# RG-LRU gates as products of 64 rows with r and i side by side, and segment differences on GpSimd

## The chip, the cores and the metric

One core of a Trainium2 chip runs one program. The metric is the device time of an execution in microseconds (us); the kernel before takes 1347.77 us, the median of 3 runs (1346.13 to 1348.24). The engines are TensorE (PE; PEld is its weight load), VectorE (DVE), ScalarE (ACT), GpSimd (POOL) and SyncE (SP), which issues the DMAs here.

## What is computed

Two layers on x (1 x 512 x 1024, float32): a recurrent layer (an RG-LRU and a Mamba-2 SSD side by side, one input and one output projection), then dilated attention, each followed by a SwiGLU feed-forward. The change touches two places of the recurrent layer:

```python
xb = xc.reshape(b, l, LRU_BLOCKS, LRU_BLOCK)                    # 16 blocks of 64 channels
r = sigmoid(einsum('blhi,hij->blhj', xb, w_r).reshape(b, l, w) + b_r)
i = sigmoid(einsum('blhi,hij->blhj', xb, w_i).reshape(b, l, w) + b_i)
log_a = -LRU_C * r * softplus(-lam)
a, u = exp(log_a), sqrt(-expm1(2.0 * log_a)) * (i * xc)         # then a scan over time: h = a * h + u
...
seg = cs[:, :, :, None] - cs[:, :, None, :]                     # SSD, chunks of 128, 16 heads
decay = exp(where(causal, seg, -inf))
```

## The kernel before

Tiles are 128 partitions (channels) by 512 columns (time). The big projections (`project`, L231; L113 to L115) multiply in three passes of float32r: each weight tile of 128x1024 is loaded (`wr`), cast by ACT to `wh` and its rest `wl` is taken on DVE (`split`, L90 and L91). `weight(i)` issues loads and splits for two tiles ahead; there are three buffers each of `wr`, `wh` and `wl`. PSUM has four buffers for projections (`pa`) and three for all else (`pm`).

The recurrent layer works through 8 tiles of each kind. For RG-LRU tile j (called block j here, two of the reference's blocks of 64): projection, a convolution over time on DVE (`conv`, L292 and L295), then `lru_act(j)`: two float32 products with `lru_w`, whose 128x128 weight tile holds the two blocks of 64 on its diagonal and zeros elsewhere (L486 for r, L488 for i), Tanh of each (L491, L492), two Exps and a Tanh on ACT (L497 to L499) and two DVE steps (L500, L501). After every four blocks `lru_end` takes one Sqrt over all four (L563) and then, block by block, a product, the scan and the gate (L506, L510, L517) on DVE and a split.

For SSD heads, two at a time (`ssd_pair`): the running sum `cs` of a head is brought by DMA to all partitions (`bcs`), ACT takes its Exp for 64 rows of `E` (L536), four DVE instructions of 128x128 subtract the column's value and clip at 0 (L540), ACT takes Exp (L541), DVE multiplies by `cb` (L542). `ssd_out` uses the result as the moving operand of `ps_yd` (L552): for each chunk two products, whose outputs lie in the lower and the upper 64 partitions of one PSUM tile. `ps_yo` (L556) are whole products of 128 columns.

What follows a projection is put on the list `held` and issued after the matmuls of the next projection. The order on each engine is not the program's order: the tile framework's planner, with its own cost of every instruction, lets an engine take the earliest instruction in the program among those that it holds ready. On the chip, each engine then keeps that order.

```python
held.append(lambda: lru_act(j, xc))                       # in lru_gates(j), after project and conv
...
for j in range(8):
    lru_gates(j)
    if j % 2 == 1:
        ssd_pair(j // 2)
        gate(4 + j // 2)
    if j % 4 == 3:
        held.append(lambda j=j: lru_end(j))
```

The other four head pairs run later, between the z projections.

Of the kernel before, what the change touches and what calls it, by code (L numbers as in the profile page):

```python
# [10 lines left out]
F32 = mybir.dt.float32  # L11
F32R = mybir.dt.float32r
AF = mybir.ActivationFunctionType
ALU = mybir.AluOpType
AX = mybir.AxisListType

P = 128
D = 1024
T = 512
NT = T // P  # L20
KD = D // P
# [37 lines left out]
def trunk(ctx: ExitStack, tc: tile.TileContext, a):  # L59
    nc = tc.nc  # L60
    mm = nc.tensor.matmul
    V, S, G = nc.vector, nc.scalar, nc.gpsimd

    def fill(pool, n):
        t = pool.tile([P, n // 4], F32, name=f"fill{n}", bufs=1)
        nc.gpsimd.memset(t[:, :1], 0.0)
# [9 lines left out]
    pm = ctx.enter_context(tc.tile_pool(name="pm", bufs=3, space=bass.MemoryType.PSUM))  # L76
# [154 lines left out]
    def project(i, hl):  # L231
        w = weight(i)
        ps = pa.tile([P, T], F32, tag="pa", name="ps_pr")
        n = len(hl)
        for k in range(n):
            mm3(ps, w, hl[k], (slice(None), slice(k * P, (k + 1) * P)), (slice(None), slice(None)), k == 0, k == n - 1)
        ready = held[:]
        held.clear()
        for f in ready:
            f()  # L240
        return ps
# [13 lines left out]
        norm.feed_sq(k)  # L255
    with ExitStack() as rctx:
        rp = rctx.enter_context(tc.tile_pool(name="rp", bufs=1))
        lru_w = rp.tile([P, 2, KD, P], F32, name="lru_w")
        fill(rp, 320)
        hp = rctx.enter_context(tc.tile_pool(name="hp", bufs=1))  # L260
        sctx = ExitStack()
# [46 lines left out]
        for j in range(4):  # L308
            ps = first[j] if j < 2 else project(i_proj[32 + j], norm.hl)
# [8 lines left out]
        ps = pm.tile([P, T], F32, tag="pm", name="ps_dtt")  # L318
        W2 = 32 + H
        for c in range(NT):  # L320
# [22 lines left out]
        br2 = rp.tile([P, 8], F32, name="br2")  # L343
        bi2 = rp.tile([P, 8], F32, name="bi2")
# [9 lines left out]
            out=adt.rearrange("p (c h) -> p c h", c=NT),  # L354
            in0=dt.rearrange("p (c h) -> p c h", c=NT),
            scalar=-1.0,
            in1=ea.rearrange("p (o h) -> p o h", o=1).to_broadcast([P, NT, H]),
            op0=ALU.mult, op1=ALU.mult,
        )
        ps = pm.tile([P, T], F32, tag="pm", name="ps_cs")  # L360
# [10 lines left out]
        ps = pm.tile([P, T], F32, tag="pm", name="ps_csT")  # L371
# [10 lines left out]
        for g in range(2):  # L382
            ps = pm.tile([P, T], F32, tag="pm", name="ps_bt")
# [5 lines left out]
            ps = pm.tile([P, T], F32, tag="pm", name="ps_cb")  # L389
            for c in range(NT):  # L390
# [4 lines left out]
                out=t.rearrange("p (c l) -> p c l", c=NT), in0=ps.rearrange("p (c l) -> p c l", c=NT),  # L395
# [60 lines left out]
        for g in range(2):  # L456
            e_t = rt2.tile([P, NT - 1, T], F32, tag="xde", name=f"xde{g}", bufs=1)
            for jj in range(4):
                j = 4 * g + jj
                ps = project(i_proj[24 + j], norm.hl)  # L460
# [17 lines left out]
        def lru_gates(j):  # L478
            ps = project(i_proj[j], norm.hl)
            xc = rt2.tile([P, T], F32, tag="xc", name="xc", bufs=4)  # L480
            conv(ps, "lconv_w", "lconv_b", j, xc)
            held.append(lambda: lru_act(j, xc))

        def lru_act(j, xc):
            pr = pm.tile([P, T], F32, tag="pm", name="ps_r")
            mm(pr, lhsT=lru_w[:, 0, j], rhs=xc, start=True, stop=True)  # L486
            pi = pm.tile([P, T], F32, tag="pm", name="ps_i")
            mm(pi, lhsT=lru_w[:, 1, j], rhs=xc, start=True, stop=True)  # L488
            tr = rt2.tile([P, T], F32, tag="tr", name="tr", bufs=1)
            ti = rt2.tile([P, T], F32, tag="ti", name="ti", bufs=1)  # L490
            S.activation(tr, pr, AF.Tanh, scale=0.5, bias=br2[:, j:j + 1])  # L491
            S.activation(ti, pi, AF.Tanh, scale=0.5, bias=bi2[:, j:j + 1])  # L492
            av = rt2.tile([P, T], F32, tag="av", name="av", bufs=4)
            if j % 4 == 0:
                lru["a2"] = rt2.tile([P, 4, T], F32, tag="a2", name="a2", bufs=1)
            a2 = lru["a2"][:, j % 4]
            S.activation(av, tr, AF.Exp, scale=ch_[:, j:j + 1], bias=ch_[:, j:j + 1])  # L497
            S.activation(a2, tr, AF.Exp, scale=cf[:, j:j + 1], bias=cf[:, j:j + 1])
            S.activation(tr, tr, AF.Tanh, scale=chn[:, j:j + 1], bias=chn[:, j:j + 1])  # L499
            V.scalar_tensor_tensor(out=a2, in0=a2, scalar=1.0, in1=tr, op0=ALU.add, op1=ALU.mult)  # L500
            V.scalar_tensor_tensor(out=xc, in0=ti, scalar=1.0, in1=xc, op0=ALU.add, op1=ALU.mult)  # L501
            lru[j] = (av, a2, xc)
# [23 lines left out]
        ck3 = cst_.rearrange("p (c h) -> p c h", c=NT)  # L526

        def ssd_pair(j):
            g, jj = j // 4, j % 4
            E = sd.tile([P, T], F32, tag="E", name="E", bufs=1)  # L530
            MT = []
            for e in range(2):
                h = 2 * j + e
                bc = sd.tile([P, T], F32, tag="bcs", name="bcs", bufs=4)
                nc.sync.dma_start(out=bc, in_=csd[h:h + 1, :].to_broadcast([P, T]))
                S.activation(E[64 * e:64 * e + 64], bc[64 * e:64 * e + 64], AF.Exp)  # L536
                sg = bc
                for c in range(NT):
                    l = slice(c * P, (c + 1) * P)
                    V.tensor_scalar(out=sg[:, l], in0=bc[:, l], scalar1=ck3[:, c, h:h + 1], scalar2=0.0, op0=ALU.subtract, op1=ALU.min)  # L540
                S.activation(sg, sg, AF.Exp)  # L541
                V.tensor_tensor(out=sg, in0=sg, in1=CB[g], op=ALU.mult)  # L542
                MT.append(sg)
            held.append(lambda: ssd_out(j, E, MT))

        def ssd_out(j, E, MT):
            g, jj = j // 4, j % 4
            pd = pm.tile([P, T], F32, tag="pm", name="ps_yd")
            for c in range(NT):
                for e in range(2):  # L550
                    s = slice(c * P, (c + 1) * P)
                    mm(pd[64 * e:64 * e + 64, s], lhsT=xdt[j][:, c, 64 * e:64 * e + 64], rhs=MT[e][:, s], start=True, stop=True)  # L552
            po = pm.tile([P, T], F32, tag="pm", name="ps_yo")
            for c in range(1, NT):
                s = slice(c * P, (c + 1) * P)
                mm(po[:, s], lhsT=prev[g, c - 1][:, jj * P:(jj + 1) * P], rhs=CT[g][:, s], start=True, stop=True)  # L556
            V.tensor_tensor(out=E[:, P:], in0=E[:, P:], in1=po[:, P:], op=ALU.mult)
            V.scalar_tensor_tensor(out=xs[j], in0=xs[j], scalar=pc("ssd_d", j), in1=pd, op0=ALU.mult, op1=ALU.add)
            V.tensor_tensor(out=xs[j][:, P:], in0=xs[j][:, P:], in1=E[:, P:], op=ALU.add)
# [8 lines left out]
# [7 lines that stand above are left out]
# [41 lines left out]
        for j in range(8):  # L616
            if j >= 4:
                ssd_pair(j)
            if j == 0:
                ps = project(i_proj[16], norm.hl)  # L620
                lctx.close()
                zctx = ExitStack()
                rt2 = zctx.enter_context(tc.tile_pool(name="zp", bufs=2))
            else:
                ps = project(i_proj[16 + j], norm.hl)
            zz = zgate(j, ps)
            zlate(j, zz)
            if j >= 3:
                out_lru(j - 3)
# [18 lines left out]
        for m in range(8):  # L648
            ps = project(i_rec[1, m], ob)
# [38 lines left out]
    with ExitStack() as actx:  # L688
# [10 lines left out]
        for w, (gn, rn, scale) in enumerate((("q_gain", "q_rope", 0.125), ("k_gain", "k_rope", 1.0))):  # L699
            g = am.tile([P, 1], F32, name=f"gain{w}", bufs=1)  # L700
# [212 lines left out]
def _chan(v):  # L913

    return v.reshape(-1, P).T
# [77 lines left out]
```

## Time and profile before

| | us | note |
|---|---|---|
| median of 3 runs | 1347.77 | 1346.13 to 1348.24 |
| the profiled execution | 1346.39 | its span 1344.6 |
| PE busy | 1318.4 | 98% of the span |
| DVE busy | 796.2 | 59% |
| ACT busy | 573.4 | 43% |
| POOL busy | 151.7 | 11% |

The times in the rows below are microseconds from the start of the span unless marked ns. L486 is line 486 of the kernel before. Busy shares are averages over stages; what a wait costs is read where it stands. Neighbours in a timeline overlap a little, since an instruction's start is pipelined with the end of the one before.

### The profile page before, as it was taken

What the parts mean: (1) busy time and instruction counts of PE and PEld (TensorE: products, weight loads), DVE (VectorE), ACT (ScalarE), POOL (GpSimd) and SP (SyncE); (2) the same over time, 40 slices, a digit from 0 to 9 for tenths busy, and PEclk for the clock granted to TensorE, in tenths of its full rate; (3) what the DMA queues carried; (4) which work ended last, traced back from release to release, by engine and by line L of the source; (5) the groups of instructions that cost most, each with busy time, mean ns of one, the idle gap of its engine ahead of it and who ended that gap; (6) DMA issues with size and microseconds to landing.
All of it is one profiled execution on the core that took longest, in us unless ns stands there. A gap on an engine that the chain in (4) does not pass through costs nothing.

```text
span 1344.6 us, 15688 instructions
## 1 busy us (share of the span) xinstructions
PE 1318.4 (98%) x6058; PEld 1072.5 (80%) x6058; DVE 796.2 (59%) x1332; ACT 573.4 (43%) x842; POOL 151.7 (11%) x130
## 2 busy tenths in 40 slices
PE   8999989999999999999999999999999999999998
PEld 6877767788888888888888877777788888888887
DVE  6886799975454434434453778788764434443442
ACT  5743867443333222322243379558643212222321
POOL 0000000000000000000005755554300000000000
PEclk9999999999999999999999999999999999999999
DMA  6322222532323323233232221121032323323232
GB/s 239 111 80 93 95 79 71 174 101 94 94 94 94 95 96 102 89 106 94 89 100 94 90 68 47 63 78 48 32 108 96 94 95 96 100 87 110 94 95 78
DMA packets 38555, 126.50 MB, mean 94 GB/s; under 512 B 4289, under 2 KB 5057, under 8 KB 38353
## 3 DMA queue, kind: packets, MB, share of 16 engines
q1 hardware_dynamic: 38480, 125.51, 29.2%
q8 instruction: 47, 0.77, 0.2%
q14 instruction: 28, 0.22, 0.0%
HBM read 123.36 MB, written 2.13 MB: 93 GB/s over the span
## 4 chain that ended last, share of the span: by engine, by line
PE 81%; DVE 9%; ACT 6%; POOL 2%; issue 1%; DMA 0%; SPq 0%; POOLq 0%; DVEq 0%; ACTq 0%
PE ps_pr L113 24%; PE ps_pr L114 24%; PE ps_pr L115 24%; ACT s L825 2%; POOL qrs L757 1%; DVE q L758 1%; PE ps_qkv L738 1%; PE ps_qkv L737 1%; PE ps_qkv L736 1%; DVE q L766 1%; ACT ph L90 1%; PE ps_o L852 1%; PE ps_pT L845 1%; ACT qk_hi L783 1%; DVE rtmp L762 1%
## 5 line engine op out<-in xcount | busy, mean ns | idle before, releaser
L90 ACT CAST wh<-wr 128x1024 fp32r<-128x1024 f32 (+2 forms) x223 | 228.2, 1025 | 621.3 <-PE ps_pr L115 388.2
L113 PE MATMUL ps_pr<-xh,wl 128*128 128x512 f32 x1056 | 416.5, 395 | 12.7 <-DVE wl L91 12.0
L114 PE MATMUL ps_pr<-xl,wh 128*128 128x512 f32 x1056 | 414.5, 392 | 0.9 <-DVE xl L191 0.9
L115 PE MATMUL ps_pr<-xh,wh 128*128 128x512 f32 x1056 | 413.2, 391 | 0.0
L91 DVE TENSOR_TENSOR wl<-wr,wh 128x1024 fp32r<-128x1024 f32 (+2 forms) x191 | 225.6, 1182 | 52.3 <-ACT wh L90 51.9
L113 PEld LDWEIGHTS ps_pr<-xh,wl 128*128 128x128 f32 x1056 | 199.4, 189 | 55.5 <-DVE wl L91 12.9
L114 PEld LDWEIGHTS ps_pr<-xl,wh 128*128 128x128 f32 x1056 | 199.5, 189 | 43.5 <-DVE xl L191 1.8
L115 PEld LDWEIGHTS ps_pr<-xh,wh 128*128 128x128 f32 x1056 | 199.3, 189 | 42.4 <-issue 0.6
L113 PE MATMUL ps_pr<-ah,wl 128*128 128x512 f32 x352 | 136.9, 389 | 0.0
L114 PE MATMUL ps_pr<-al,wh 128*128 128x512 f32 x352 | 136.9, 389 | 0.0
L115 PE MATMUL ps_pr<-ah,wh 128*128 128x512 f32 x352 | 136.9, 389 | 0.0
L91 POOL TENSOR_TENSOR wl<-wr,wh 128x1024 fp32r<-128x1024 f32 x32 | 78.4, 2453 | 392.3 <-ACT wh L90 392.2
L670 DVE TENSOR_TENSOR tu<-ps_pr,nrb 128x512 f32<-128x512 f32 x44 | 30.4, 691 | 130.7 <-PE ps_pr L115 130.7
L678 DVE TENSOR_TENSOR x<-ps_pr,x 128x512 f32<-128x512 f32 x48 | 33.2, 692 | 120.4 <-PE ps_pr L115 120.3
L668 DVE TENSOR_TENSOR tg<-ps_pr,nrb 128x512 f32<-128x512 f32 x44 | 30.4, 691 | 94.1 <-PE ps_pr L115 94.1
L114 PEld LDWEIGHTS ps_pr<-al,wh 128*128 128x128 f32 x352 | 66.1, 188 | 13.8
L115 PEld LDWEIGHTS ps_pr<-ah,wh 128*128 128x128 f32 x352 | 66.1, 188 | 13.7
L113 PEld LDWEIGHTS ps_pr<-ah,wl 128*128 128x128 f32 x352 | 66.1, 188 | 13.7
L736 PE MATMUL ps_qkv<-wh,xl 128*128 128x512 f32 x192 | 75.6, 394 | 0.5 <-ACT q L750 0.5
L737 PE MATMUL ps_qkv<-wl,xh 128*128 128x512 f32 x192 | 75.5, 393 | 0.0
L738 PE MATMUL ps_qkv<-wh,xh 128*128 128x512 f32 x192 | 75.5, 393 | 0.0
L736 PEld LDWEIGHTS ps_qkv<-wh,xl 128*128 128x128 f32 x192 | 36.1, 188 | 7.9 <-ACT q L750 1.0
(233 smaller groups left out, 1575.2 us busy)
## 6 DMA issues: line engine op xcount, KB each, us to landing
wr<-in_w_gu SPq DMA_DIRECT2D x88, 512.0 KB, 3.5
wr<-in_w_in SPq DMA_DIRECT2D x35, 512.0 KB, 3.5
wr<-in_w_dn SPq DMA_DIRECT2D x32, 448.0 KB, 3.2
wr<-in_w_qkv SPq DMA_DIRECT2D x24, 512.0 KB, 3.5
wr<-in_w_out SPq DMA_DIRECT2D x16, 512.0 KB, 3.5
wr<-in_w_dn SPq DMA_DIRECT2D x16, 512.0 KB, 3.4
x<-in_xT SPq DMA_DIRECT2D x16, 256.0 KB, 3.7
bcs<-csd SPq DMA_DIRECT2D x16, 256.0 KB, 4.4
```

The costliest lines, as they stand in the source:

```text
L90: S.copy(hi, src)
L91: eng.tensor_tensor(out=lo, in0=src, in1=hi.bitcast(F32), op=ALU.subtract)
L113: mm(ps, lhsT=wl[ws], rhs=xh[xs], start=start, stop=False)
L114: mm(ps, lhsT=wh[ws], rhs=xl[xs], start=False, stop=False)
L115: mm(ps, lhsT=wh[ws], rhs=xh[xs], start=False, stop=stop)
L668: V.tensor_tensor(out=tg, in0=pg, in1=rb, op=ALU.mult)
L670: V.tensor_tensor(out=tu, in0=pu, in1=rb, op=ALU.mult)
L678: V.tensor_tensor(out=x[m], in0=ps, in1=x[m], op=ALU.add)
L736: mm(pss[t], lhsT=xl[:, ts_], rhs=wh[:, cols], start=(k == 0), stop=False)
L737: mm(pss[t], lhsT=xh[:, ts_], rhs=wl[:, cols], start=False, stop=False)
L738: mm(pss[t], lhsT=xh[:, ts_], rhs=wh[:, cols], start=False, stop=(k == KD - 1))
L825: S.activation(s, s, AF.Exp, scale=-1.0, bias=m[:, 0:1], accum_out=m[:, 1:2])
```

## The change

The weight tile of block j is now 64 rows for each of its two blocks, with r and i beside each other in the columns: rows 0 to 63 hold (w_r, w_i) of the first block, rows 64 to 127 hold (w_i, w_r) of the second. Each product has 64 rows and gives r of one block in one half of the partitions and i in the other, in its own PSUM tile. Tanh is taken half by half: `tr` from the halves that hold r, `ti` across the halves. The bias of i is stored with its halves exchanged. `lru_w` is half as large. And the four segment differences of each head are issued on POOL (`G`) and no longer on DVE (`V`).

```diff
-        lru_w = rp.tile([P, 2, KD, P], F32, name="lru_w")
+        lru_w = rp.tile([P, KD, P], F32, name="lru_w")
...
-            pr = pm.tile([P, T], F32, tag="pm", name="ps_r")
-            mm(pr, lhsT=lru_w[:, 0, j], rhs=xc, start=True, stop=True)
-            pi = pm.tile([P, T], F32, tag="pm", name="ps_i")
-            mm(pi, lhsT=lru_w[:, 1, j], rhs=xc, start=True, stop=True)
+
+            ps = [pm.tile([P, T], F32, tag="pm", name="ps_ri") for _ in range(2)]
+            own = [slice(64 * e, 64 * e + 64) for e in range(2)]
+            for e in range(2):
+                mm(ps[e], lhsT=lru_w[own[e], j], rhs=xc[own[e]], start=True, stop=True)
             tr = rt2.tile([P, T], F32, tag="tr", name="tr", bufs=1)
             ti = rt2.tile([P, T], F32, tag="ti", name="ti", bufs=1)
-            S.activation(tr, pr, AF.Tanh, scale=0.5, bias=br2[:, j:j + 1])
-            S.activation(ti, pi, AF.Tanh, scale=0.5, bias=bi2[:, j:j + 1])
+            for e in range(2):
+                S.activation(tr[own[e]], ps[e][own[e]], AF.Tanh, scale=0.5, bias=br2[own[e], j:j + 1])
+            for e in range(2):
+                o = own[1 - e]
+                S.activation(ti[own[e]], ps[e][o], AF.Tanh, scale=0.5, bias=bi2[o, j:j + 1])
...
-    blk = np.zeros((2, 8, P, P), f)
-    for g, w in enumerate((n["lru_w_r"][0], n["lru_w_i"][0])):
-        for b in range(16):
-            o = 64 * (b % 2)
-            blk[g, b // 2, o:o + 64, o:o + 64] = w[b]
+    w_r, w_i = (n[k][0].reshape(8, 2, 64, 64) for k in ("lru_w_r", "lru_w_i"))
+
+    blk = np.concatenate([np.concatenate([w_r[:, 0], w_i[:, 0]], axis=2), np.concatenate([w_i[:, 1], w_r[:, 1]], axis=2)], axis=1)
...
-                    V.tensor_scalar(out=sg[:, l], in0=bc[:, l], scalar1=ck3[:, c, h:h + 1], scalar2=0.0, op0=ALU.subtract, op1=ALU.min)
+                    G.tensor_scalar(out=sg[:, l], in0=bc[:, l], scalar1=ck3[:, c, h:h + 1], scalar2=0.0, op0=ALU.subtract, op1=ALU.min)
```

## Rows read from the trace of the kernel before

**Rows 1.** Busy time by stretches: the stretch, its length, busy time (and instructions) of each engine, granted clock.

```profile
134.20:148.70 14.50, 14.50 (x73) 10.80 (x73) 10.71 (x18) 14.36 (x18) 0.00 (x0) 1.00 0.24 73
148.70:157.80 9.10, 9.10 (x37) 6.55 (x36) 9.05 (x18) 5.76 (x10) 0.00 (x0) 1.00 0.14 58
157.80:170.50 12.70, 12.70 (x68) 9.71 (x67) 7.50 (x17) 12.56 (x15) 0.00 (x0) 1.00 0.41 126
...
189.50:217.80 28.30, 28.30 (x138) 20.45 (x137) 25.40 (x44) 27.31 (x35) 0.00 (x0) 1.00 0.40 130
...
229.00:330.00 101.00, 100.71 (x508) 82.55 (x509) 77.30 (x133) 42.48 (x61) 2.02 (x2) 1.00 0.39 125
```

**Rows 2.** Waits, 55 to 300: who waited for whom, us in total, times, longest.

```profile
PE ps_pr L113 <- DVE wl L91: 6.1, 2, 4.6
...
PEld ps_yd L552 <- ACT ti L492: 1.5, 2, 0.8
...
ACT tr L491 <- DVE a L500: 0.6, 1, 0.6
```

**Rows 3.** Chain of waits: start, us on the chain, what.

```profile
168.60 1.93 ACT a L563
...
181.12 1.15 DVE wl L91
182.31 0.80 PE ps_pr L113
...
209.18 0.58 ACT tr L491
...
215.86 1.93 ACT a L563
...
228.97 0.50 PE ps_pr L113
```

**Rows 4.** The same view, products of TensorE.

```profile
137.06 0.86 PE ps_i L488 x2
137.92 1.02 PE ps_yd L552 x16
140.30 0.67 PE ps_yo L556 x6
...
275.75 0.86 PE ps_yo L556 x6
```

**Rows 5.** Timeline of TensorE: start, us from first start to last end, instruction, count.

```profile
137.85 0.33 PE L552 MATMUL ps_yd<-bcs,xdt 128*64 128x128 f32 x2
```

**Rows 6.** Groups of ACT's instructions, 126 to 300: count, busy us, mean ns.

```profile
L536 ACT ACTIVATE E<-bcs 64x512 f32<-64x512 f32 x14 | 8.8, 629 | 10.0 <-DVE xs L559 9.8
L541 ACT ACTIVATE bcs<-bcs 128x512 f32<-128x512 f32 x14 | 8.7, 628 | 1.6 <-DVE bcs L540 1.5
```

**Rows 7.** Timeline of DVE.

```profile
205.67 1.26 DVE L540 TENSOR_SCALAR bcs<-bcs,csk 128x128 f32<-128x128 f32 x6
```

**Rows 8.** Groups of POOL's instructions by form.

```profile
L827 POOL TENSOR_SCALAR s<-s,m 128x384 f32<-128x384 f32 x16 | 9.8, 610 | 6.3 <-DVE m L826 4.8 <-ACT ph L90 1.5
...
L827 POOL TENSOR_SCALAR s<-s,m 128x128 f32<-128x128 f32 x16 | 6.4, 399 | 8.1 <-DVE m L826 8.1
```

**Rows 9.** Timeline of ACT.

```profile
201.84 0.63 ACT L536 ACTIVATE E<-bcs 64x512 f32<-64x512 f32 x1
...
207.11 1.14 ACT L541 ACTIVATE bcs<-bcs 128x512 f32<-128x512 f32 x2
...
214.57 1.28 ACT L563 ACT_TABLE_LOAD   x1
```

**Rows 10.** Timelines of POOL and of DVE in the attention.

```profile
744.23 2.88 DVE L758 TENSOR_TENSOR q<-q,qrs 128x512 f32<-128x512 f32 x1 [1.53 <-POOL qrs L757]
...
834.68 0.67 DVE L758 TENSOR_TENSOR q<-q,qrs 128x512 f32<-128x512 f32 x1
...
834.85 0.95 POOL L827 TENSOR_SCALAR s<-s,m 128x384 f32<-128x384 f32 x1 [0.17 <-DVE m L826]
```

**Rows 11.** Busy time by stretches, columns as in rows 1.

```profile
182.30:185.20 2.90, 2.89 (x7) 2.31 (x8) 2.90 (x6) 0.00 (x0) 0.00 (x0) 0.50 0.48 175
```

More of the change, by code (lines that the diff above doesn't have):

```diff
@@ L961 @@
         "lconv_w": conv(n["lru_conv_w"][0]), "lconv_b": _chan(n["lru_conv_b"][0]),
-        "b_r": _chan(n["lru_b_r"][0]), "b_i": _chan(n["lru_b_i"][0]), "lam": _chan(n["lru_lambda"][0]),
+        "b_r": _chan(n["lru_b_r"][0]), "b_i": _chan(n["lru_b_i"][0].reshape(8, 2, 64)[:, ::-1].reshape(-1)), "lam": _chan(n["lru_lambda"][0]),
         "sconv_w": conv(n["ssd_conv_w"][0]), "sconv_b": _chan(n["ssd_conv_b"][0]),
@@ L975 @@
         "w_dt": w_in[:, 4608:].reshape(8, P, 16).transpose(1, 0, 2),
-        "lru_w": blk.transpose(2, 0, 1, 3),
+        "lru_w": blk.transpose(1, 0, 2),
         "w_out": np.stack([_tiles(n["rec_w_out"][0][h * D:(h + 1) * D], 8) for h in range(2)]),
```

## The prediction

> **What bounds the kernel now.** The page's busy times, in the table above, come first: TensorE is busy 98% of the span, so a microsecond counts only if it shortens TensorE's work or one of its waits. Then the busy time by stretches, where the changed lines run. TensorE is full nearly everywhere, but ScalarE (ACT) is busy 14.36 of 14.50 us while blocks 0 and 1 of the RG-LRU go through, 12.56 of 12.70 around block 3 and 27.31 of 28.30 for blocks 4 to 7; between, from 148.7 to 157.8, it has 3.3 us of air. After 229 TensorE has next to none (100.71 of 101) [rows 1]. The waits tell where these stages touch TensorE: two waits, 4.6 and 1.5 us, for `wl`, the low part of a weight tile, made on VectorE (DVE) [rows 2]. The chain of waits shows what lies behind both: a run of ACT work ends in the Sqrt of L563, the scans of four blocks follow on DVE, `wl` stands among their last, and TensorE goes on at 182.31 and 228.97 [rows 3]. In this stage the path is ACT, then DVE; TensorE's products beside it are cover.
>
> **The change, step by step.** *Products.* A float32 product of 512 columns is two passes, 0.86 us in the chain, so r and i of a block cost 1.72 us [rows 4]. The new ones use 64 rows each, on different halves. The nearest row is `ps_yd`, on halves of the columns: two passes that take 0.33 us each are over in 0.33 us together [rows 5], and its sixteen take 1.02 us, where six whole passes of the same length (`ps_yo`) take 0.67, 0.11 each. Eight slots of 0.11 make 0.88, so 0.14 is entry; leaving costs 0.19, the difference between `ps_yo` right behind `ps_yd` (0.86) and elsewhere (0.67) [rows 4]. If halves of the rows run as halves of the columns do, a block costs 0.86 + 0.14 + 0.19 = 1.19 us, 0.53 less. In blocks 1, 3 and 7 the products stand right before `ps_yd`, which pays the way out already (rows 4 begin with one of the three): there it is 0.72. Blocks 4 and 5 come back to back before `ps_yd` and save 3.44 - 1.86 = 1.58. Together 3 x 0.53 + 3 x 0.72 + 1.58 = 5.3 us of TensorE work. Bounds: if nothing overlaps, entry and exit are added, 3 x 0.33 + 4 x 0.14 = +1.6 us; if of four passes only the middle two overlap, the saving is 5.3 - 8 x 0.43 = 1.9. I take 5.3, because the nearest row has pairs.
>
> By the Trainium skill, "TensorE: Matmul & The Clock Gate", section "Part 3: Packing small matmuls — row/col tiling", products on different rows of the array run at once, but matmuls start and end strictly in program order. If both passes of one half are issued before those of the other, that rule gives the saving of 1.9 us; `ps_yd` shows pairs from its first two passes on, and no row here shows a half of the rows.
>
> *Tanh.* Two activations per block become four, on 64 partitions each. Partitions don't set the time: 64x512 takes 629 ns on average, 128x512 628 [rows 6]. Back to back, a Tanh out of PSUM moves the chain by 0.58 us [rows 3], so a block adds 1.16 us to ACT, and all eight 9.3. Where do they lie? Blocks 0 to 2 add 3.5 us between 134 and 157.8, where ACT has 0.14 + 3.34 us of air [rows 1]; TensorE is a little ahead by then, so the air can be used, and next to nothing is late. Block 3 is in a full stretch: its Sqrt comes some 1.4 us later. The scans behind it are DVE work that loses nothing by the change, so `wl` and TensorE's restart move with it, to about 183.7. Blocks 4 to 7 add 4.64 us where there is 1.0 of air [rows 1], of which 0.6 is ACT's own wait for `a` (`tr` has one buffer) and is filled [rows 2]; 4.1 stay. The second Sqrt is late by 1.4 + 4.1 = 5.5 us, and with it the scans, `wl` and TensorE's restart at 228.97.
>
> *Segment differences.* 64 instructions leave DVE, at 0.21 us each (six in a row take 1.26) [rows 7]: 13.4 us of DVE time. On the path there is none of it: no L540 lies between a Sqrt and the `wl` after it, and the eight pieces of heads 6 and 7, the last of them in rows 7, are done while ACT is busy. On GpSimd (POOL) the nearest instruction, the attention's TENSOR_SCALAR of 128x128, takes 399 ns [rows 8]; eight are 3.2 us. ACT's Exp of `E` for head 7 starts at 201.84 and the Exps of the differences at 207.11 [rows 9]: 5.3 us, so POOL is hidden. The upper bound of a piece: a 128x384 one took 0.95 us beside a DVE product that read two inputs from SBUF, 0.34 more than the mean of its form [rows 8, 10]; with that on each, eight make 5.9 us, 0.6 more than the cover. Lower than nothing it can't be on this path, since ACT sets it. After 229 TensorE waits for next to nothing [rows 1], so the DVE time saved in the other eight heads brings nothing; the small `pow` of the group norm, on POOL too, could queue behind two pieces, 0.8 us.
>
> *Halved `lru_w`.* It is loaded once, long before its first use at 133 us, and nothing waits for it: nothing.
>
> **Sum.** TensorE's 5.3 us lie in front of two waits that others end: it arrives earlier and stands longer. Behind 229 it is full, so what counts is the second restart: +5.5 us. Then the clock. TensorE's idle 4.6 us before 182.31 [rows 2] was followed by 2.9 us at a granted clock of 0.50, the lower level (1.2 GHz) [rows 11], which costs 1.45 us. With TensorE 2.8 us quicker over blocks 4 to 7 (0.53 + 0.72 + 1.58) and the restart 4.1 us later against the first, the second idle becomes 1.5 + 2.8 + 4.1 = 8.4 us, and in one piece would bring another fall, +1.45. I leave that out of the value, because part of it should be spent earlier in short waits: the PSUM tiles of r and i are now held to the third and fourth Tanh, and `ps_yd` already waited for the end of `ti` [rows 2]. The profiled execution, 1346.4 us, goes to 1351.9; the median lies 1.4 above it, so I forecast **1353.3 us**, for this case alone 1350.8 (+3, if the planner uses more of ACT's air) to 1357 (+9, with the clock and POOL's 0.6 and 0.8).
>
> **Rivals.**
> 1. *TensorE's saving shows (not slower).* Where `wl` stands among the scans is planned, not given. If with Sqrt later the planner puts the second `wl` ahead of the scans, TensorE doesn't wait there and goes by its own work: first restart +1.4, blocks 4 to 7 -2.8, second wait -1.5: -2.9 on 1347.8, 1344.9 us. If the first `wl` moves too, that wait shrinks as well, but block 7's products still stand behind ACT and DVE, so not far below 1341. For it: DVE waits for Sqrt in both places, and `wl` would fit there. Against: in both places the cast that `wl` needs came behind Sqrt on ACT, and a fuller ACT has fewer gaps. It decides once that cast stands ahead of Sqrt.
> 2. *ACT takes them up (no change).* Four table loads of 1.28 us, the last of them in rows 9, lie in the stretch of blocks 4 to 7. If ACT's new order saves one there and one around block 3, and uses all air, the second restart is 5.5 - 2.6 - 0.4 = 2.5 us late; if the PSUM waits split the idle so that no clock falls at all, 1.45 comes back: +1.0, about 1348.8 us.
> 3. *POOL and DVE block one another (slower still).* A DVE product with both inputs in SBUF took 2.88 us beside a TENSOR_TENSOR on POOL, where another of the same form took 0.67 [rows 10]. If each of the eight pieces at 201 to 207 holds a DVE instruction for its 0.40 us, the DVE steps between ACT's are 3.2 us late in the full stretch: 5.5 + 3.2, 1356.5 us. It decides if TENSOR_SCALAR shuts DVE out as TENSOR_TENSOR does; the 0.67 was taken beside the piece of 0.95, so there POOL waited and DVE did not.
>
> The Trainium skill's "GPSIMD Engine Reference", section "8. Key points", says that POOL contends with DVE instructions that have two SBUF inputs, which most of DVE's here have; by it rival 3 would hold. Rows 10 agree for TENSOR_TENSOR, and for TENSOR_SCALAR only on POOL's side.
>
> **How the numbers follow.** Forecast 0.5, rival 1 0.2, rival 2 0.2, rival 3 0.1. A difference of 0.2%, 2.7 us, is about what a measurement of this kernel tells from no change; the bounds are 1345.1 and 1350.5. Faster: 0.15 (three quarters of rival 1). Same: the rest of rival 1 (0.05) and most of rival 2 (0.18), 0.23. Slower: 0.62. The range, 1344.5 to 1357.5 us, leaves out the deeper half of rival 1 and the ends of forecast and rival 3.
>
> **What would show it.** The products: four passes of 64 rows per block, starting in pairs 0.43 us apart. Tanh: 32 of 64x512, ACT without air from 190 to 223, the Sqrts at about 170 and 221. TensorE's waits for `wl`: two, together above 12 us. POOL: 64 pieces, 25 us or more. I am wrong if `wl` stands ahead of the scans, if the second Sqrt starts before 219 us, or if TensorE waits elsewhere before 330 us for more than 2 us.

## The result, and the profile after

The changed kernel takes 1379.39 us (median of 4 runs, 1378.06 to 1380.06), the kernel before beside it 1346.95 us (4 runs, 1346.13 to 1348.24): a ratio of 1.0233, 95% interval 1.0219 to 1.0248. The forecast was 1353.3 us with a range up to 1357.5: the sign was right, the size wrong by a factor of nearly six, 32 us in place of 5.5.

| | before | after |
|---|---|---|
| the profiled execution, us | 1346.39 | 1380.06 |
| its span | 1344.6 | 1378.3 |
| PE busy | 1318.4 | 1331.8 |
| span less PE busy | 26.2 | 46.5 |
| POOL busy | 151.7 | 209.9 |
| first DVE instruction of the first feed-forward (`tg`) starts at | 370.8 | 402.8 |

Nearly all of the loss lies before the first feed-forward, which starts 32.0 us later; from there to the end the two differ by 1.7. Of the 33.7 us of span, 20.3 are idle time of TensorE and 13.4 are busy time that got longer, though the products themselves became shorter. The stretches of [rows 1] at the same times, though some of the work has moved behind them, and the whole of 55 to 340 us; columns as there:

```profile
134.20:148.70 14.50, 14.06 (x73) 9.97 (x72) 9.75 (x15) 11.55 (x15) 0.00 (x0) 1.00 0.12 40
...
157.80:170.50 12.70, 9.54 (x47) 6.92 (x46) 8.16 (x12) 11.30 (x16) 4.53 (x5) 0.87 0.41 124
189.50:217.80 28.30, 25.46 (x99) 16.71 (x97) 23.33 (x36) 16.14 (x22) 3.90 (x4) 0.82 0.27 88
229.00:330.00 101.00, 89.52 (x428) 72.29 (x427) 69.59 (x99) 46.36 (x63) 31.60 (x34) 0.92 0.34 107
55.00:340.00 285.00, 258.62 (x1174) 199.83 (x1174) 199.40 (x282) 157.28 (x201) 62.71 (x66) 0.94 0.28 91
```

Two things are to be seen. ACT is no longer full from 189.5 to 217.8 (16.14 of 28.30 us, 27.31 before). In part this is a shift, since its first Tanh of block 4 starts at 198.08 and no longer at 190.44, and only 3.3 us of its waits in this stretch are for POOL. And TensorE has lost its cover from 229 to 330 us, 11.5 us idle there (0.3 before), in a stretch where the prediction expected no cost but that of a small `pow`; with the idle time the granted clock falls, to 0.82 and 0.92 of full speed on average (1.00 before in both stretches). The waits, 55 to 300 us, as in [rows 2], say who waits:

```profile
ACT bcs L545 <- POOL bcs L544: 30.0, 10, 6.2
DVE bcs L546 <- ACT bcs L545: 18.2, 10, 3.4
...
PE ps_pr L113 <- DVE wl L91: 7.8, 3, 3.4
...
PE ps_yd L556 <- DVE bcs L546: 6.4, 4, 2.2
```

The first line did not exist before; in its place ACT waited 5.1 us in all for the same pieces on DVE. Now the Exp of the differences (L545 now, L541 before) waits 30 us for POOL's pieces (L544, before L540). The page's groups give the price of a piece, then the timeline of POOL three stretches of pieces:

```profile
L544 POOL TENSOR_SCALAR bcs<-bcs,csk 128x128 f32<-128x128 f32 x64 | 59.7, 949 | 210.8 <-ACT E L540 203.4
```

```profile
172.85 2.78 POOL L544 TENSOR_SCALAR bcs<-bcs,csk 128x128 f32<-128x128 f32 x4 [10.52 <-ACT E L540]
179.61 6.00 POOL L544 TENSOR_SCALAR bcs<-bcs,csk 128x128 f32<-128x128 f32 x4 [3.98 <-ACT E L540]
...
245.73 6.04 POOL L544 TENSOR_SCALAR bcs<-bcs,csk 128x128 f32<-128x128 f32 x4 [6.91 <-ACT E L540]
```

Four pieces at 172.85 take 0.70 us each; four at 179.61 and four at 245.73, both beside scans and two-input products of the RG-LRU blocks on DVE, take 1.5 each. The prediction had 0.40. How such a stretch reaches TensorE is read from the timelines at 245 to 261 us, of DVE, then ACT, then TensorE:

```profile
245.71 2.33 DVE L514 TENSOR_TENSOR_SCAN hs<-av,xc 128x512 f32<-128x512 f32 x2
247.96 1.32 DVE L521 TENSOR_TENSOR oat<-gg,hs 128x512 f32<-128x512 f32 x2
...
253.92 1.29 DVE L91 TENSOR_TENSOR oal<-oat,oah 128x512 fp32r<-128x512 f32 x2 [3.42 <-ACT oah L90]
...
258.74 1.22 DVE L91 TENSOR_TENSOR wl<-wr,wh 128x1024 fp32r<-128x1024 f32 x1
```

```profile
251.80 0.63 ACT L545 ACTIVATE bcs<-bcs 128x512 f32<-128x512 f32 x1 [6.16 <-POOL bcs L544]
252.34 1.03 ACT L90 CAST wh<-wr 128x1024 fp32r<-128x1024 f32 x1
253.27 1.13 ACT L90 CAST oah<-oat 128x512 fp32r<-128x512 f32 x2
```

```profile
260.01 0.50 PE L113 MATMUL ps_pr<-xh,wl 128*128 128x512 f32 x1 [2.12 <-DVE wl L91]
```

ACT stands 6.16 us before one Exp. Behind it in ACT's order are a cast `wh` and the casts `oah`; for `oah` DVE stands 3.42 us; behind DVE's rests `oal` is, in the end, `wl`, and for that TensorE stands 2.12 us. The wait is put down to `wl`, and its cause is POOL, three engines away. In the z phase the chain shows the same, POOL, ACT, DVE and TensorE in turn, the first time without a weight tile between:

```profile
281.12 4.23 POOL bcs L544 x6
...
285.38 0.64 ACT bcs L545
...
286.04 0.70 DVE bcs L546
...
286.79 1.97 PE ps_yd L556 x14
...
307.97 4.94 POOL bcs L544 x7
...
315.49 1.13 DVE wl L91
...
326.83 0.43 PE ps_pr L114
...
329.65 0.24 PE ps_pr L115
```

The last two lines are the clock: a product of the same size moves the chain by 0.43 us after the idle time before it, at the lower level (1.2 GHz), and by 0.24 three microseconds later, at 2.4 GHz.

### The profile page after: what moved, and what is told of

It is laid out like the page before. It is cut to its first block, busy times and chain, and to the rows that moved or that the text cites. A ratio compares the mean times of both kernels' runs of the same rounds, so it can differ in the third digit from the quotient of the medians.

```text
span 1378.3 us, 15742 instructions
## 1 busy us (share of the span) xinstructions
PE 1331.8 (97%) x6058; PEld 1078.3 (78%) x6058; DVE 787.6 (57%) x1268; ACT 585.7 (42%) x859; POOL 209.9 (15%) x194
## 4 chain that ended last, share of the span: by engine, by line
PE 63%; DVE 8%; ACT 4%; POOL 2%; issue 2%; POOLq 0%; DVEq 0%; ACTq 0%
PE ps_pr L113 19%; PE ps_pr L114 19%; PE ps_pr L115 19%; DVE q L762 2%; ACT s L829 1%; POOL qrs L761 1%; POOL bcs L544 1%; PE ps_qkv L741 1%; PE ps_qkv L742 1%; PE ps_qkv L740 1%; DVE q L770 1%; ACT ph L90 1%; PE ps_pT L849 1%; PE ps_o L856 1%; ACT qk_hi L787 1%
## 5 line engine op out<-in xcount | busy, mean ns | idle before, releaser
L544 POOL TENSOR_SCALAR bcs<-bcs,csk 128x128 f32<-128x128 f32 x64 | 59.7, 949 | 210.8 <-ACT E L540 203.4
```

The source lines that it names most:

```text
L544: G.tensor_scalar(out=sg[:, l], in0=bc[:, l], scalar1=ck3[:, c, h:h + 1], scalar2=0.0, op0=ALU.subtract, op1=ALU.min)
```

## The experiments

Theory at the start: the pieces on POOL make the loss, by their price; the gates do what was predicted. Rivals: the gates on a later Sqrt; POOL and DVE shutting each other out; the order that the planner makes around POOL. Line numbers in the edits are those of the kernel before or after; times are medians, each ratio with its 95% interval.

**One half of the change alone.** e1_pool_only is the kernel before with the pieces on POOL, e2_gates_only the changed kernel with them on DVE:

```diff
-                    V.tensor_scalar(out=sg[:, l], in0=bc[:, l], ...)
+                    G.tensor_scalar(out=sg[:, l], in0=bc[:, l], ...)
```

> The segment differences on POOL alone, gate products and Tanh as before. Theory A (the POOL pieces are the cause: 0.71 us each where nothing else runs, up to 2.7 us beside DVE, and they stand in the chain Exp of E, four pieces, Exp, product, ps_yd): most of the 32 us is here, 1371 to 1380 us, mean piece 0.9 to 1.0 us, TensorE waiting at ps_yd and for wl. Theory B (four half Tanhs on a full ACT and PSUM tiles held longer are the cause): 1345 to 1352 us.

> The 64-row gate products and the half Tanhs alone, segment differences on DVE as before. Theory A: close to the kernel before; by the terms of the prediction (5.3 us less TensorE work, restart behind the second Sqrt 5.5 us later) 1346 to 1354 us. Theory B: 1365 to 1380 us.

Measured: e1 1380.39 us, 1.0241 (1.0225 to 1.0256); e2 1352.91 us, 1.0034 (1.0021 to 1.0047), both against 1348.3. The pieces alone make the whole loss, +32.1 us, and the gates on top of them nothing; the gates alone cost 4.6. e1 lies 0.4 above the range expected, with a mean piece of 0.88, a little below the 0.9 to 1.0. The waits of e1, 55 to 340 us:

```profile
ACT bcs L541 <- POOL bcs L540: 37.2, 15, 3.8
...
PE ps_pr L113 <- DVE wl L91: 14.2, 2, 7.2
```

ACT's timeline of e1 shows how the wait moves the Sqrt. Between 140 and 176 us it stands for POOL twice for long:

```profile
156.45 0.63 ACT L541 ACTIVATE bcs<-bcs 128x512 f32<-128x512 f32 x1 [3.82 <-POOL bcs L540]
...
174.09 0.63 ACT L541 ACTIVATE bcs<-bcs 128x512 f32<-128x512 f32 x1 [2.72 <-POOL bcs L540]
...
176.69 1.92 ACT L563 ACTIVATE a<-a 128x2048 f32<-128x2048 f32 x1
```

Together 6.5 us of the 8.1 by which this Sqrt is late (168.60 before, [rows 3]); scans, `wl` and TensorE's restart follow it. The second Sqrt is 19.4 us late (235.3), with 7.1 us more of waits for POOL between the two.

**The price of a piece, by itself.** e3_probes puts groups of four TENSOR_SCALAR on POOL into each of two stages where POOL is idle, with other operations and sizes:

```diff
+            for _ in range(4):
+                G.tensor_scalar(out=pb[:, :128], in0=lnc[:, T - 128:], scalar1=sc, scalar2=0.0, op0=ALU.subtract, op1=ALU.min)
+            for _ in range(4):
+                G.tensor_scalar(out=pb[:, :128], in0=lnc[:, T - 128:], scalar1=sc, scalar2=1.0, op0=ALU.mult, op1=ALU.mult)
...
```

> The kernel before, with POOL instructions added in the feed-forward stages where POOL is idle: TENSOR_SCALAR on 128x128 with (subtract, min), (mult, mult), (subtract, mult), (mult, min), (subtract alone), (add, min), then (subtract, min) and (mult, mult) on 128x512. Theory A1 (the operations set the time of a piece): (subtract, min) about 0.71 us and (mult, mult) about 0.37 to 0.40 us, the others telling whether min or subtract costs. Theory A2 (all forms alike; what surrounds the pieces slows them): both about 0.40 us. The time of the kernel stays at 1345 to 1352 us.

The groups by line, with the shortest, the median and the longest duration in ns: (subtract, min) and (mult, mult) on 128x128, subtract alone, then the first two pairs on 128x512:

```profile
L665 POOL TENSOR_SCALAR pb<-cst,nrt x8: 712/713/717, 366.8 to 994.3; 128x128 f32<-128x128 f32 x8
L667 POOL TENSOR_SCALAR pb<-cst,nrt x8: 372/374/1272, 370.0 to 997.4; 128x128 f32<-128x128 f32 x8
L673 POOL TENSOR_SCALAR pb<-cst,nrt x8: 602/603/1738, 380.2 to 1007.5; 128x128 f32<-128x128 f32 x8
L677 POOL TENSOR_SCALAR pb<-cst,nrt x8: 1994/1998/3522, 387.4 to 1021.5; 128x512 f32<-128x512 f32 x8
L679 POOL TENSOR_SCALAR pb<-cst,nrt x8: 692/694/1766, 397.1 to 1027.0; 128x512 f32<-128x512 f32 x8
```

Its time as a whole, 1348.96 us in one run, is that of the kernel before. The operations set the price, not the size alone: 374 ns for (mult, mult), 713 for (subtract, min) on the same tile; per added column 0.83 and 3.35 ns (694 - 374 and 1998 - 713 over 384). The attention's instruction of [rows 8], 399 ns, is a (mult, mult). (subtract, mult), (mult, min) and (add, min) took 714 to 720 too.

**The price inside the kernel.** e4_pool_multmult is e1 with another pair of operations, so that the decays are others:

```diff
-                    G.tensor_scalar(..., scalar2=0.0, op0=ALU.subtract, op1=ALU.min)
+                    G.tensor_scalar(..., scalar2=-1.0, op0=ALU.mult, op1=ALU.mult)
```

> As the POOL-only kernel, but each piece computes (value times scalar) times -1 instead of (value minus scalar) clipped at 0; the decays are then other numbers. Theory A1 (operations set the piece): pieces of 0.40 us alone, and the loss shrinks to a third or less, 1347 to 1358 us. If the blocking between POOL and DVE products of two SBUF inputs is what costs: the mean piece stays above 0.7 us and the time above 1365 us.

Measured: 1361.38 us, 1.0099 (1.0085 to 1.0113). The instructions of e4 and e1 stand in the same order on every engine, so the 19.0 us between them are the price of 64 pieces alone, and the planner, which made one order for both, does not see that price. 13.1 us stay, 41% of the loss, where a third or less was expected; 1361 lies between the ranges of the two theories. The tile's row of e4 has the median, 372 ns; the groups of e4 and then e1 have the means, and ACT's waits of e4 stand last:

```profile
L540 POOL TENSOR_SCALAR bcs<-bcs,csk x64: 364/372/1851, 63.7 to 296.0; 128x128 f32<-128x128 f32 x64
```

```profile
L540 POOL TENSOR_SCALAR bcs<-bcs,csk 128x128 f32<-128x128 f32 x64 | 35.6, 575 | 212.6 <-ACT E L536 206.7
```

```profile
L540 POOL TENSOR_SCALAR bcs<-bcs,csk 128x128 f32<-128x128 f32 x64 | 55.2, 878 | 208.2 <-ACT E L536 200.7
```

```profile
ACT bcs L541 <- POOL bcs L540: 19.9, 14, 3.1
```

The means lie above the undisturbed 374 and 713 ns of e3 by 0.20 and 0.17 us a piece, 13 and 11 us for all 64: what stretches the pieces inside the kernel takes about as much from the cheap ones. And e4 has, undisturbed, the price that the prediction took for a piece, and still loses 13.1 us. The wrong price alone is not the whole error.

**Part of the pieces.** e7_pool_first8 moves heads 0 to 7 only, e8_pool_last8 heads 8 to 15 (the z phase), e13_half_pieces two of the four pieces of every head:

```diff
+                    (G if j < 4 else V).tensor_scalar(...)       # e7
...
+                    (V if j < 4 else G).tensor_scalar(...)       # e8
...
+                    (V if c < 2 else G).tensor_scalar(...)       # e13
```

> The segment differences on POOL for heads 0 to 7 only (beside the RG-LRU blocks), gates as before. If the pieces cost through the full run of ACT and DVE behind the two Sqrts, two thirds of the 32 us are here, 1366 to 1374 us. If they cost through ps_yd, which waits for the slow chain of each pair, a third, 1355 to 1362 us.

> The segment differences on POOL for heads 8 to 15 only (between the z projections, where TensorE had no wait). The prediction held that nothing there hangs on them: 1346 to 1350 us. If the chain E, eight pieces of 0.71 us, Exp, product is longer than a projection, TensorE waits at ps_yd: 1354 to 1362 us.

> The kernel before with two of the four segment differences of each head on POOL, the other two on VectorE. Theory (POOL's rate against the cover of 5.3 us per pair of heads): four pieces of 0.71 to 0.95 us are 2.8 to 3.8 us per pair, inside the cover, so ScalarE waits for POOL less than 6 us in all (37 with all pieces) and the time is 1347 to 1352 us. Rival (each piece blocks or delays a VectorE step, or the order planned around POOL is the worse one): the loss goes with the number of pieces, half of 32 us, 1364 us, with 15 us or more of ScalarE's waits for POOL.

Measured: e7 1358.96 us, 1.0087 (1.0073 to 1.0101); e8 1358.72, 1.0079 (1.0064 to 1.0094); e13 1355.27, 1.0050 (1.0036 to 1.0064). ACT's waits for POOL in the three, in this order:

```profile
ACT bcs L541 <- POOL bcs L540: 15.7, 7, 3.8
```

```profile
ACT bcs L541 <- POOL bcs L540: 20.3, 8, 3.9
```

```profile
ACT bcs L541 <- POOL bcs L540: 9.7, 8, 1.9
```

Half of the pieces of each head cost a fifth of the loss (6.9 of 32 us), half of the heads a third. That fits a cost by how far POOL's queue for one head outlasts its cover, and does not show it, since the order is planned anew in each run. e7 and e8 came out in the ranges that were tied to `ps_yd`, but not by that way: TensorE waits at `ps_yd` for the decays 0.4 us in e7 and at most 3.0 in e8. In e7 the Sqrts are 7.1 and 15.4 us late and TensorE waits for `wl` and for the convolution's `xc`, in e8 for `wl` and for the sum `gacc` of the group norm. Neither theory of e13 had it: 1355 lies outside the 1347 to 1352 of the cover and far from the 1364 of a loss by the piece. e7 and e8 add up to 21.5 us, not 32; what the two halves cost together beyond that, some 10 us, was not taken apart further.

**More cover for the same pieces.** e14_exp_later issues the Exp and the product behind it one projection later (and the pairs of the z phase one projection earlier); e15_exp_later_dve is the same with the pieces on DVE:

```diff
-                S.activation(sg, sg, AF.Exp)
-                V.tensor_tensor(out=sg, in0=sg, in1=CB[g], op=ALU.mult)
...
+            def decays():
+                for sg in MT:
+                    S.activation(sg, sg, AF.Exp)
+                    V.tensor_tensor(out=sg, in0=sg, in1=CB[g], op=ALU.mult)
+                held.append(lambda: ssd_out(j, E, MT))
+            held.append(decays)
```

> All pieces on POOL as in the change, products as before; but the Exp of the differences and the product on VectorE behind it are issued one projection later (and the pairs of the z phase one projection earlier), so that POOL has a projection of about 5.5 us more for its eight pieces of a pair. Theory (ScalarE's in-order queue waits at the Exp because POOL is late, and that is the loss): the waits of ScalarE for POOL fall from 37 us to under 8, and the time to 1348 to 1356 us. Rival (pieces on POOL cost by blocking VectorE wherever they stand): waits at the Exp go, the time stays above 1365 us.

> The same later Exp, with the segment differences on VectorE as in the kernel before: the base for the run with POOL and a later Exp. Theory: VectorE's pieces were in time anyway, so the move brings nothing or costs some by another order: 1345 to 1352 us. Rival (the Exp stood on ScalarE's path to the Sqrt, and later it stands behind it): the second Sqrt starts 1 us or more earlier and the time falls to 1343 to 1345 us.

Measured: e14 1368.53 us, 1.0146 (1.0133 to 1.0160); e15 1347.52, 0.9993 (0.9984 to 1.0002). The move brings back 12 of the 32 us, and my reason for it fell: ACT's waits for POOL are the same. The time is above the theory's range, and the rival, by which these waits go, does not hold either.

```profile
ACT bcs L545 <- POOL bcs L540: 36.9, 15, 3.9
```

The program's order gave a projection of air, and in the planned order the Exp again stands on ACT before POOL is done. The waits cost less where they stand now: TensorE's waits for `wl` are 3.0 us in all, 14.2 in e1, and why they do was not taken apart.

**The gates apart.** e5_gates_two_tanh is e2 with two whole Tanhs, so that r and i are mixed up in half of the channels; e6_half_tanh is the kernel before with its Tanhs halved:

```diff
-            for e in range(2):
-                S.activation(tr[own[e]], ps[e][own[e]], AF.Tanh, ...)
...
+            S.activation(tr, ps[0], AF.Tanh, ...)                # e5; ti from ps[1]
...
-            S.activation(tr, pr, AF.Tanh, ...)
+            for e in range(2):
+                S.activation(tr[own[e]], pr[own[e]], AF.Tanh, ...)   # e6; ti likewise
```

> The 64-row gate products alone, but with two Tanhs of all 128 partitions as before, so that r and i are mixed up in half of the channels; segment differences on DVE. Theory C (the 4.6 us that the gates alone cost come from the two added Tanhs per block on a full ACT): back to the kernel before or below it, 1343 to 1349 us. Rival D (the products themselves cost: entry and exit of the array's modes, slower passes, PSUM tiles held longer): 1350 us or more.

> The kernel before with each Tanh of r and i taken in two halves of 64 partitions: 16 more activations, the products as before. Theory C: ACT's full stretches grow as with the gates, TensorE restarts 4 to 6 us later, 1351 to 1355 us. Rival D: ACT's air takes the Tanhs up, 1346 to 1349 us.

Measured: e5 1345.81 us, 0.9986 (0.9978 to 0.9995); e6 1355.66, 1.0059 (1.0046 to 1.0071). The halves of Tanh cost 7.6 us (1355.66 lies 0.7 above the range expected), and the products bring 2.3 by the medians (1.9 by the ratio, 0.7 to 3.0 by its interval).

**A version that wins?** e9_early_tile lets `lru_end` issue one weight tile more ahead of its scans, in the kernel before; e10_gates_early_tile does it in e2.

```diff
         def lru_end(j):
...
+            emit_to(emitted[0])
```

> The kernel before, with one more weight tile (load, cast, rest) issued at the start of lru_end, so that the planner ranks it ahead of Sqrt and the scans. If the order on DVE (wl behind the four scans) makes the two waits of TensorE, they shrink from 6.1 us together, and the clock doesn't fall: 1339 to 1344 us. If the DVE and ACT work itself is the bound, wherever wl stands, the waits come back later: 1346 to 1350 us.

> The 64-row gates (differences on DVE) with the weight tile issued at the start of lru_end. If TensorE's saved work shows once it doesn't wait behind the scans: 2 to 5 us below the kernel before with the same early tile, 1336 to 1342 us. If ACT's added Tanhs hold TensorE at the products and at ps_yd all the same: 1344 us or more, and no faster than the kernel before with the early tile.

Measured: e9 1348.17 us, 1.0004 (0.9995 to 1.0013); e10 1359.80, 1.0088 (1.0074 to 1.0102). In e9 the waits for `wl` fall to 3.8 us in all, from 6.1 [rows 2], and nothing comes of it; in e10 the second Sqrt slips to 231.4 us (225.1 in e2). Both expectations of a gain failed; both runs lie in the ranges of their second cases (1346 to 1350, and 1344 or more). In e9 the second Sqrt is itself 1.9 us later (217.8). The cast and rest that now come earlier are in ACT's and DVE's way, which I read from e10's Sqrt and did not test.

e11_quadrants and e12_four_quadrants keep r and i of both blocks together, so that Tanh stays whole, by products of 64 rows and 64 columns: e11 on two quarters of the array at a time, e12 on four, with DVE's L501 in two halves.

```diff
-            for e in range(2):
-                mm(ps[e], lhsT=lru_w[own[e], j], rhs=xc[own[e]], start=True, stop=True)
+            for g, ps in enumerate((pr, pi)):
+                for e in range(2):
+                    mm(ps[own[e]], lhsT=lru_w[own[e], j, own[g]], rhs=xc[own[e]], start=True, stop=True)
```

> Segment differences on VectorE, as before; the products of a block as four of 64 rows and 64 columns on the two diagonal quarters of the array (r of both blocks into one PSUM tile, i of both into another), so that Tanh stays whole, two per block, and everything that is computed is the reference's. Theory (the gates' loss is the halved Tanh alone, and products on row halves bring their 1.9 us): as the run with two whole Tanhs, about 1346.2 us, ratio 0.9985, the second Sqrt near 215, eight product slots of 0.5 us per pair of passes: about 1.0 us of slots and 0.4 us of way in and out for each block. Rival (quarters of the array don't run beside each other, each product then has its own two passes): eight passes of 0.43 us, 3.4 us per block in place of 1.7, +13 us of TensorE work, of which at least 6 show: 1354 us or more. Second rival (two products that write one PSUM bank take turns there): the same sign, about 1350.

> The same, but on all four quarters of the array: i of a block goes to the other half of the PSUM partitions, Tanh stays whole, and the VectorE step of L501 is done in two halves across the partitions. Theory (what sets the time of this stage is ScalarE and then the scans): TensorE's four products at once save a further 0.5 us or more per block, but VectorE has 0.6 us more per block, 4.8 us in all, part of it ahead of the scans: between 1345 and 1350 us, no better than the run on two quarters. Rival (TensorE's work is what counts here): 4 us or more below the run on two quarters, 1342 us.

Measured: e11 1352.33 us, 1.0027 (1.0016 to 1.0037); e12 1349.87, 1.0013 (1.0004 to 1.0022). The timeline of TensorE in e11, in e12, and in the changed kernel:

```profile
133.01 1.08 PE L491 MATMUL ps_r<-xc,lru_w 64*64 64x512 f32 x4
133.89 1.05 PE L491 MATMUL ps_i<-xc,lru_w 64*64 64x512 f32 x4
134.87 0.50 PE L113 MATMUL ps_pr<-xh,wl 128*128 128x512 f32 x1
```

```profile
132.86 0.65 PE L491 MATMUL ps_r<-xc,lru_w 64*64 64x512 f32 x2
...
133.35 0.60 PE L491 MATMUL ps_i<-xc,lru_w 64*64 64x512 f32 x2
```

```profile
212.89 0.39 PE L115 MATMUL ps_pr<-xh,wh 128*128 128x512 f32 x1
213.21 1.13 PE L489 MATMUL ps_ri<-xc,lru_w 64*128 64x512 f32 x4
214.27 0.50 PE L113 MATMUL ps_pr<-xh,wl 128*128 128x512 f32 x1
```

My expectation for e11 had miscounted: eight passes in pairs are four slots of about 0.44 us, 1.86 us from the first start to the next projection, no less than the two whole products (1.72). The two rivals are not seen either, since the quarters do run in pairs, also into one PSUM tile. But 0.14 us a block is 1.1 in all, and e11 is 4.0 slower. Its second Sqrt stands at 219.8 (215.9 before) with whole Tanhs: block 4 starts 2.0 us later, and an Exp for `E`, with a table load of its own, was planned ahead of the Sqrt, 1.9 us. So the planned order alone can be worth a few us in any of these runs, and a difference of that size is not shown to be the edit's own. In e12 all four quarters run at once and the eight passes start within 0.5 us; the time lies in the range of the theory, no better than before and by the medians 2.5 below e11, and I put that down to the halves on DVE, which no run shows by itself. No version here is shown to beat the kernel before: e5 is 2.3 us below, and computes something else.

## Why the prediction was wrong

The starts of the two Sqrts, which the prediction named as its sign, in us, and the time against the kernel before beside each:

| kernel | first Sqrt | second Sqrt | time |
|---|---|---|---|
| before [rows 3] | 168.6 | 215.9 | |
| forecast | 170 | 221 | +5.5 |
| e2, gates alone | 169.4 | 225.1 | +4.6 |
| e5, gates with whole Tanhs | 166.8 | 215.1 | -2.3 |
| e6, Tanhs halved alone | 170.1 | 222.8 | +7.6 |
| e11, products on two quarters | 169.2 | 219.8 | +4.0 |
| e1, pieces alone | 176.7 | 235.3 | +32.1 |
| e4, pieces of (mult, mult) | 170.5 | 226.1 | +13.1 |
| e7, pieces of heads 0 to 7 | 175.7 | 231.3 | +10.9 |
| e8, pieces of heads 8 to 15 | 168.6 | 217.3 | +10.6 |
| e14, later Exp | 173.9 | 229.5 | +20.2 |
| after | 174.1 | 236.7 | +32.4 |

*The segment differences: here it failed.* The sentence was "On GpSimd (POOL) the nearest instruction, the attention's TENSOR_SCALAR of 128x128, takes 399 ns". It was nearest in engine, kind and size, and not in its operations: 0.71 us without any neighbour (e3), 0.95 in the kernel. Eight pieces are then 5.7 us undisturbed and 7.6 as measured, against the cover of 5.3 [rows 9], and "so POOL is hidden" falls with it. It would not have held at the assumed price either: e4 loses 13.1 us at 0.37 us a piece undisturbed, 0.58 on average. Of the prediction's own signs of being wrong, the last came true: TensorE waits 6.4 us at `ps_yd` for the decays. The upper bound, 0.74, was about the price of an undisturbed piece; it was built from contention, which came on top.

The Trainium skill, "GPSIMD Engine Reference", section "4.1 Engine selection", says that elementwise work with one input runs at roughly line rate on GpSimd. The runs bear this out for (mult, mult), 694 ns for 128x512, close to ACT's Exp of that size (628, [rows 6]); for (subtract, min), also one tensor input, the 1998 ns measured decide against it.

*Rivals 1 and 2* are excluded by the time, and by the order: `wl` stands behind the scans both times (at 186.26 behind a scan that starts at 185.03, at 249.20 behind those of 245.71), and ACT has five table loads from block 4 to the second Sqrt, where it had four.

*POOL and DVE (rival 3).* The rival put the delay on DVE's side, 3.2 us in all. The trace shows it mainly on POOL's side: four pieces take 2.78 us at 172.85 and 6.00 at 179.61, where DVE's products, rests and scans run one behind another; DVE's own product L546 takes 743 ns on average where it took 686 (L542 before), 0.9 us for all 16, while the 64 pieces lose 15 ((949 - 713) x 64).

The Trainium skill, "GPSIMD Engine Reference", section "8. Key points", names contention with DVE instructions that have two SBUF inputs; these numbers agree, for TENSOR_SCALAR too.

*The cover, and what stands behind it.* The prediction asked what hides the pieces at 201 to 207 us and what one piece too long would cost there, 0.6 us. It did not ask what is queued behind the Exp on ACT in the order that would be planned: the Sqrt, the casts of weights, and so scans, `wl` and TensorE. The same 37 us of ACT's waits went with a loss of 32 us in e1 and of 20 in e14, in another order; which of the things behind them makes the difference is not shown. And the order is planned with a price that doesn't know the operation (e1 and e4 have one order).

*The z phase.* "After 229 TensorE waits for next to nothing, so the DVE time saved in the other eight heads brings nothing." The first half was true of the kernel before; e8 shows that these eight heads alone cost 10.6 us, with the Sqrts hardly moved. A saving that brings nothing was looked at, a cost in the same place was not.

*The clock.* One more fall, +1.45, was weighed and left out. With 20 us more of idle time the granted clock averages 0.94 over 55 to 340 us, and 13.4 us of the loss are busy time. That is the second term that was missed, and it follows from the first.

*The gates: right in kind, near in size by luck.* Tanh: 32 instructions of 64x512, 681 and 683 ns on average, no shorter than whole ones; alone they cost 7.6 us (e6), against the 5.5 of the forecast's mechanism, and the second Sqrt came 6.9 us later, against 5.5. One term was too small: the halves follow one another at 0.70 us, as in these lines of the changed kernel, and not at the 0.58 of a whole one [rows 3].

```profile
164.53 0.68 ACT L496 ACTIVATE ti<-ps_ri,bi 64x512 f32<-64x512 f32 x1
165.23 0.68 ACT L493 ACTIVATE tr<-ps_ri,br 64x512 f32<-64x512 f32 x1
```

Four halves for two whole ones are then 1.64 us a block and not 1.16. The 1.4 us for the first Sqrt does not follow from the 1.16 of block 3; it moved by 0.8 in e2 and 1.5 in e6. The link from Sqrt to time was looser than forecast: in e2 the second Sqrt is 9.2 us late and the time only +4.6; TensorE's waits for `wl` there are three, 5.2 us in all, where two above 12 were named as the sign. That the gates' cost came out near the forecast is therefore luck: a second Sqrt later than forecast and a looser link offset one another, in an order that was not the one worked out.

Products: a block takes 1.06 us from its first start to the next projection's, after an entry of 0.09 (0.32 in place of 0.23), 1.15 together, where 1.19 was worked out from the halves of the columns; of the 5.3 us forecast, 2.3 reach the end in e5. Not every block runs so: at 217.9 TensorE waits 2.3 us for `ti` between the two halves, one of the short waits for PSUM that the prediction named. `lru_w`: nothing was found to wait for it. With the gates on top of the pieces (after against e1) there is no further loss; that ACT waits for POOL anyway, 35.3 us there and 37.2 in e1 over 55 to 340 us, fits this and was not tested.

*Open.* Of the 32 us, 19 are the price of the operations (e4). The cause of the other 13 stays open. Candidates are that pieces beside DVE's work take longer (0.58 us in place of 0.37) and the order planned around POOL; they were not taken apart, since the order can't be held while the engine changes.

## What to carry to other kernels

An instruction's price is that of its operations: before work is moved to another engine, find a row there with the same operations, and where none is, put the doubling into the range. An in-order engine that waits for a slower one holds up everything queued behind the wait, so ask not only for the excess over the cover but for what stands behind it, in the order as it will be. And a stretch where TensorE is full is no licence: a saving on another engine may bring nothing there, while a delay can stop TensorE (10.6 us in e8) and cost again in the clock.

## What was not expected of the hardware

On POOL a TENSOR_SCALAR of 128x128 takes 374 ns with (mult, mult), 603 with a subtract alone, and 713 to 720 with every other pair tried; at 128x512 it is 694 against 1998. Float32 products of 64 rows do run in pairs on the halves of the rows, and four at a time on the quarters of the array, also into one PSUM tile; the two pairs of the block shown above start 0.53 us apart, the pairs on quarters 0.43 to 0.48, where whole passes are 0.43 apart [rows 4].
